# A second feed-forward chunk by seven block products, with the first chunk's up units between them

## The chip, the cores and the metric

The kernel runs on one core of a Trainium2 chip. The metric is device time in microseconds (us) of one execution; lower is better. A profiled execution gives a trace of every engine: TensorE (PE, with its weight loads as PEld), VectorE (DVE), ScalarE (ACT), GpSimd (POOL) and SyncE (SP, which here only issues DMAs).

## The reference

A trunk of two layers over 256 positions of width 1024, float32. Each layer is

```
h = rms_norm(x, ln1_g)
proj = h @ w_in                         # three token mixers and their gates
x = x + merged_mixers(proj) @ w_o
h2 = rms_norm(x, ln2_g)
x = x + (silu(h2 @ w_ff_gate) * (h2 @ w_ff_up)) @ w_ff_down     # 1024 -> 2816 -> 1024
```

The change touches only the last line, the SwiGLU feed-forward part, once in each layer.

## The kernel before

**Precision and products.** Every weight tile and every activation tile is kept as a high and a low part (`wh`, `wl` and `ah`, `al`, both float32r). A 128x128 by 128x512 product is three matmuls: high by high, high by low, low by high (`products`, L308 to L310).

**Weight units.** Weights come in units of 512 KB. SP loads a unit into one of six `st` tiles (L253); ScalarE copies it to `wh` (L272) and VectorE subtracts to get `wl` (L273), each in one of five ring tiles; TensorE then uses it. `loads` is the order of the loads, `cuts` the order of the splits, and both are written out by `plan` before anything else; `take` gives the next unit. A unit of a gate or up projection holds 256 rows by 512 columns and serves 12 matmuls (2 row tiles of 128 positions, 2 row blocks of the weight, 3 matmuls). A unit of the down projection also serves 12.

**The feed-forward part.** Its 2816 hidden columns are five chunks of 512 and one of 256. An ordinary chunk is eight units: four of the gate projection into two PSUM banks, four of the up projection into two more; then silu, the product, four transposes for each row tile and the split into `hsets`. The down units of a chunk follow the gate and up units of the next one (the chunk's hidden part is ready by then). The four down accumulators stand in the four `acc` banks over the whole part; the chunks use the four `tp` banks, except chunk 0, which uses `acc` banks, since the down sums haven't begun.

**Chunks by seven products** (`SEVEN`, chunks 2 and 4 before). Gate and up side by side make a matrix of 2 by 2 blocks (row halves of the weight by gate/up); the activations are 2 by 2 blocks too (two row tiles by two halves of the width). `seven` multiplies these with seven block products instead of eight, in Winograd's form: it needs four combinations of activation blocks (`block_sums`: sums on GpSimd, then splits on ScalarE and VectorE) and four of weight blocks. The weight combinations are made by DMA: base units are loaded (`x` into the two tiles that held `merged`, `y` into those that held `qz`), and GpSimd issues accumulating DMAs that add another block from HBM onto the same tile (L276). The two `x` units are split four times, with one more block added after each of the first three. A block product uses a unit for 6 matmuls. In between, `seven` takes the four down units of the chunk before it at three places: one, two, one.

**What sets the order.** Code is traced in order, with a small list of side tasks (`flow`) that move one step on at each "atom" (6 matmuls); the compiler's scheduler then places each instruction on its engine's queue as early as its operands, its tile and the trace's priorities let it. So a load of the x or y tiles that stands late in the trace can be issued much earlier, once its tile is free. Each engine's queue is then in order.

**Lines that matter here:** L272, L273 the splits; L253 the loads; L276 the accumulating DMAs; L953 and L959 the activation sums, L962 and L963 their splits; L993 the copy of a block sum (`part`), L997, L1014 and L1017 the additions and subtractions of block sums; L977 the hidden product of a seven-product chunk, L929 that of an ordinary one; L336 the transposes; L940 silu.

Of the kernel before, what the change touches and what calls it, by code (L numbers as in the profile page):

```python
# [18 lines left out]
P = 128  # L19
D = 1024  # L20
# [15 lines left out]
NW = 512  # L36
# [4 lines left out]
STAGES = 6  # L41
AHEAD = 5
RING = 5
SEVEN = (2, 4)
LAST = 4

R_CONV, R_CB, R_BA, R_BI, R_LAM, R_SGB, R_QG, R_KG, R_SUB, R_END = (
# [57 lines left out]
def trunk(ctx: ExitStack, tc: tile.TileContext, a: dict, onehot: bass.AP, out: bass.AP):  # L105
# [14 lines left out]
    flow = Flow()  # L120
# [14 lines left out]
    def rows(w, k0, k, c0, c1):  # L135
        return w[k0 * P:(k0 + k) * P, c0:c1].rearrange("(k p) n -> p k n", p=P)
# [14 lines left out]
    def plan(l):  # L151
        def cut(parts):
            cuts.append((unit(parts), []))

        def cols(w, c, n=4):
            for u in range(n):
                cut([(0, NW, rows(w, 2 * u, 2, c * NW, (c + 1) * NW))])

        def down_cut(k):
            cut([(0, D, wd[k * P:(k + 1) * P, :].unsqueeze(1))])  # L160

        def seven(c):

            def half(w, kh):
                return [rows(w, 4 * kh + 2 * u, 2, c * NW, (c + 1) * NW) for u in range(2)]
            b11, b21 = (half(a["w_ff_gate"][l], kh) for kh in range(2))
            b12, b22 = (half(a["w_ff_up"][l], kh) for kh in range(2))
            ks = iter(range(4 * c - 4, 4 * c))
            x = [unit([(0, NW, b11[u])], "merged") for u in range(2)]
            y = [unit([(0, NW, b12[u])], "qz") for u in range(2)]  # L170
            cuts[-1][1].extend((y[u], b22[u]) for u in range(2))
            cuts.extend((x[u], [(x[u], b12[u])]) for u in range(2))
            for u in range(2):
                cut([(0, NW, b21[u])])
            down_cut(next(ks))
            cuts.extend((x[u], [(x[u], b22[u])]) for u in range(2))
            down_cut(next(ks))
            down_cut(next(ks))
            cuts.extend((x[u], [(x[u], b21[u])]) for u in range(2))
            for u in range(2):  # L180
                cut([(0, NW, b22[u])])
            cuts.extend((y[u], []) for u in range(2))
            down_cut(next(ks))
            cuts.extend((x[u], []) for u in range(2))

        w_in, wd = a["w_in"][l], a["w_ff_down"][l]
        for c in (C_XG, C_UV, C_Q, C_K, C_V):
            cols(w_in, c)
        for g in gates_order:
            if isinstance(g, tuple):  # L190
                cols(w_in, C_GATE + 2 * g[0] + g[1])
            else:
                n = int(g[-1])
                cols(a["w_pa"][l], n, 1)
                cols(a["w_pb"][l], n, 1)
                cols(a["w_pc"][l], n, 2)
        for n in range(2):
            cols(a["w_o"][l], n)
        for c in range(nfull + 1):
            if c in SEVEN:  # L200
                seven(c)
                continue
            if c < nfull:
                cols(a["w_ff_gate"][l], c)
                cols(a["w_ff_up"][l], c)
            else:
                lo, hi = c * NW, FFN
                for u in range(4):
                    cut([(0, rest, rows(a["w_ff_gate"][l], 2 * u, 2, lo, hi)),
                         (rest, 2 * rest, rows(a["w_ff_up"][l], 2 * u, 2, lo, hi))])  # L210
            if c:
                for k in range(4 * c - 4, 4 * c):
                    down_cut(k)
        for k in range(4 * nfull, nk_down):
            down_cut(k)
# [93 lines left out]
        nc.tensor.matmul(acc, ah[:, k, :], wl[:, kk, cols], start=False, stop=False, **kw)  # L309
        state["pe"] = nc.tensor.matmul(acc, al[:, k, :], wh[:, kk, cols], start=False, stop=last, **kw).ins  # L310

    def project(sets, nunits, acc):

        for u in range(nunits):
            w = take()
            for r in range(NR):
                for kk in range(2):
                    k = 2 * u + kk
                    products(acc[r], sets[r][k // 4], k % 4, w, kk, slice(0, NW),
                             k == 0, k == 2 * nunits - 1)  # L320
                if r == NR - 1:
                    release()
                atom_done()

    def accs():
        return [acc_bank() for _ in range(NR)]
# [471 lines left out]
    def layer(l, norm1, operands, acc=None):  # L798
# [182 lines left out]
            hsets[c, r] = split(tp, 4)  # L981
            yield 1

        def seven(c):


            (a11, a12), (_, a22) = norm2.sets
            ks = iter(range(4 * c - 4, 4 * c))
            x, w = tp_bank(0), tp_bank(1)

            def copy(bank):
                t = t2k("part")
                nc.scalar.activation(t, bank, AF.Copy)  # L993
                return t

            def gate0(t):
                nc.vector.tensor_tensor(t, t, w, ALU.add)  # L997
                nc.scalar.activation(t, t, AF.Silu, scale=rstd2[0])
                yield 1

            block(x, a11, True)
            g0 = copy(x)
            block(w, a12, True)
            flow.start(gate0(g0))
            down_units([next(ks)])
            z = tp_bank(2)
            block(z, s_ops["s1"], True)
            u1 = copy(z)
            down_units([next(ks)])
            down_units([next(ks)])  # L1010
            block(x, s_ops["s2"], False)
            u0 = copy(x)
            block(z, s_ops["s4"], False)
            nc.vector.tensor_tensor(u0, z, u0, ALU.subtract)  # L1014
            flow.add(half_hidden(c, 0, u0, g0), 1)
            block(x, s_ops["s3"], False)
            nc.vector.tensor_tensor(u1, u1, x, ALU.subtract)  # L1017
            down_units([next(ks)])
            block(x, a22, False)
            g1 = t2k("sg")  # L1020
            nc.scalar.activation(g1, x, AF.Silu, scale=rstd2[1])
            return flow.add(half_hidden(c, 1, u1, g1), 1)
# [24 lines left out]
        def down_units(ks):  # L1047
            if not downs:
                for n in range(2):
                    for r in range(NR):  # L1050
                        downs[r, n] = acc_bank()
            for k in ks:
                w = take()
                for n in range(2):
                    for r in range(NR):
                        down(k, w, r, n)
                    if n == 1:
                        release()
                    atom_done()
# [25 lines left out]
            yield 1  # L1085
            yield from nxt.halves(n)

        flow.add(block_sums(), 18)
        th = None
        for c in range(nfull + 1):  # L1090
            if c in SEVEN:
                th = seven(c)
                continue
            if th is not None and c - 1 in SEVEN:
                before = th
                th = gate_up(c)
                flow.finish(before)
            else:
                th = gate_up(c)
            if 1 <= c < nfull:  # L1100
                down_units(range(4 * c - 4, 4 * c))
                flow.finish(th)
# [171 lines left out]
```

## Time and profile before

| what | value |
|---|---|
| median of 3 runs | 755.29 us (753.62 to 755.35) |
| the profiled execution | 753.26 us, span 751.5 us, granted clock 1.0 |
| TensorE busy | 741.1 us (99%), 3425 matmuls and transposes |
| weight loads busy | 608.3 us (81%) |
| VectorE / ScalarE / GpSimd busy | 530.8 / 438.8 / 148.0 us |
| DMA | 157.70 MB, mean 210 GB/s |

Layer 0's feed-forward part runs from about 199 to 386 us of the span, layer 1's from about 566 us to the end. Busy shares are means over stages with different limits. Matmuls are pipelined, so that their durations overlap; how long a stretch of them takes is read from windows.

### The profile page before, as it was taken

The numbers are of one execution on the slowest core, as the hardware profiler recorded it, in microseconds if no ns is written. First come the engines' busy times: TensorE is split into PE (matmuls) and PEld (weight loads), VectorE is DVE, ScalarE is ACT, GpSimd is POOL, SyncE is SP. The second block draws the span as 40 slices with busy tenths as digits, with TensorE's granted clock in tenths as the row PEclk, the third lists the DMA queues.
The fourth block names the chain that finished last, engine by engine and source line by source line (L and its number), as shares of the span: only waits on it lengthen the run. The fifth ranks groups of instructions, "written<-read, shape, count | busy, mean of one in ns | idle before, by whom it ended". The sixth has DMA issues, their size and how long they took to land.

```text
span 751.5 us, 9745 instructions
## 1 busy us (share of the span) xinstructions
PE 741.1 (99%) x3425; PEld 608.3 (81%) x3425; DVE 530.8 (71%) x749; ACT 438.8 (58%) x647; POOL 148.0 (20%) x163
## 2 busy tenths in 40 slices
PE   8998999999999999999999999999999999999997
PEld 5787888888888887888888788888888888788886
DVE  5788977677785667559577968676866855946772
ACT  5649765454764565457486966554457545745650
POOL 1543010401360211120011420222107211102100
PEclk9999999999999999999999999999999999999999
DMA  6995668677656799888655558776575669997931
GB/s 206 338 313 171 205 191 233 208 218 232 191 167 200 174 239 341 218 213 247 191 175 164 169 166 219 200 225 196 181 240 170 195 171 224 292 314 176 246 116 57
DMA packets 79020, 157.70 MB, mean 210 GB/s; under 512 B 6086, under 2 KB 11836, under 8 KB 78972
## 3 DMA queue, kind: packets, MB, share of 16 engines
q1 hardware_dynamic: 68844, 136.48, 56.3%
q0 software_dynamic: 10128, 20.60, 15.4%
q8 instruction: 27, 0.44, 0.2%
q14 instruction: 21, 0.17, 0.1%
HBM read 156.00 MB, written 1.84 MB: 210 GB/s over the span
## 4 chain that ended last, share of the span: by engine, by line
PE 82%; DVE 6%; DMA 5%; issue 2%; POOL 2%; ACT 2%; SPq 1%; ACTq 0%; DVEq 0%; POOLq 0%
PE acc L310 18%; PE acc L308 18%; PE acc L309 18%; PE tp L308 8%; PE tp L310 8%; PE tp L309 8%; DMA st<-in_w_in_dram 3%; PE tp L336 3%; DVE wl L273 2%; ACT wh L272 2%; PE tp L727 1%; DMA st<-in_w_ff_up_dram 1%; POOL rr L360 1%; DMA st<-in_w_ff_gate_dram 1%; PE tp L762 1%
## 5 line engine op out<-in xcount | busy, mean ns | idle before, releaser
L273 DVE TENSOR_TENSOR wl<-st,wh 128x1024 fp32r<-128x1024 f32 (+1 forms) x277 | 342.3, 1244 | 173.2 <-ACT wh L272 171.8
L272 ACT ACTIVATE wh<-st 128x1024 fp32r<-128x1024 f32 (+1 forms) x277 | 289.5, 1055 | 218.3 <-PE acc L310 119.2
L308 PE MATMUL acc<-wh,ah 128*128 128x512 f32 x704 | 282.4, 401 | 0.0
L310 PE MATMUL acc<-wh,al 128*128 128x512 f32 x704 | 275.3, 391 | 0.0
L309 PE MATMUL acc<-wl,ah 128*128 128x512 f32 x704 | 274.7, 390 | 0.4 <-DVE cqz L468 0.4
L310 PEld LDWEIGHTS acc<-wh,al 128*128 128x128 f32 x704 | 132.1, 188 | 28.2
L309 PEld LDWEIGHTS acc<-wl,ah 128*128 128x128 f32 x704 | 132.5, 188 | 26.3 <-DVE cqz L468 0.9
L308 PEld LDWEIGHTS acc<-wh,ah 128*128 128x128 f32 x704 | 132.3, 188 | 26.0 <-issue 0.6
L308 PE MATMUL tp<-wh,ah 128*128 128x512 f32 x208 | 82.1, 395 | 0.8 <-DVE part L1017 0.8
L310 PE MATMUL tp<-wh,al 128*128 128x512 f32 x208 | 81.1, 390 | 0.0
L309 PE MATMUL tp<-wl,ah 128*128 128x512 f32 x208 | 81.0, 389 | 0.0
L276 POOL DMA_DIRECT2D st<-in_w_ff_up_dram x24 | 28.9, 1222 | 176.5 <-DVE wl L273 163.8
L308 PEld LDWEIGHTS tp<-wh,ah 128*128 128x128 f32 x208 | 39.1, 188 | 8.9 <-issue 1.2
L310 PEld LDWEIGHTS tp<-wh,al 128*128 128x128 f32 x208 | 39.0, 188 | 8.3
L309 PEld LDWEIGHTS tp<-wl,ah 128*128 128x128 f32 x208 | 39.1, 188 | 7.7
L381 POOL TENSOR_TENSOR nss<-nsq 128x1 f32<-128x1 f32 x8 | 3.6, 447 | 123.0 <-ACT junk L377 123.0
L853 POOL TENSOR_TENSOR merged<-merged,tg 128x512 f32<-128x512 f32 x12 | 19.2, 1622 | 39.4 <-DVE tg L850 39.4
L310 PE MATMUL tp<-wh,sl 128*128 128x512 f32 x64 | 25.2, 394 | 0.0
L309 PE MATMUL tp<-wl,sh 128*128 128x512 f32 x64 | 25.2, 394 | 0.0
L308 PE MATMUL tp<-wh,sh 128*128 128x512 f32 x64 | 25.2, 393 | 0.0
L888 POOL DMA_DIRECT2D bg<-in_b_gate_dram x12 | 7.1, 592 | 91.3 <-DVE tg L841 91.3
L342 ACT ACTIVATE ah<-tp 128x512 fp32r<-128x512 f32 (+1 forms) x32 | 17.9, 560 | 9.0 <-PE tp L336 9.0
(203 smaller groups left out, 662.1 us busy)
## 6 DMA issues: line engine op xcount, KB each, us to landing
st<-in_w_in_dram SPq DMA_DIRECT2D x87, 512.0 KB
st<-in_w_ff_down_dram SPq DMA_DIRECT2D x44, 512.0 KB
st<-in_w_ff_up_dram SPq DMA_DIRECT2D x40, 512.0 KB
st<-in_w_ff_gate_dram SPq DMA_DIRECT2D x40, 512.0 KB
st<-in_w_ff_up_dram POOLq DMA_DIRECT2D x24, 512.0 KB, 6.7
st<-in_w_o_dram SPq DMA_DIRECT2D x16, 512.0 KB
st<-in_w_pc_dram SPq DMA_DIRECT2D x8, 512.0 KB
st<-in_w_ff_gate_dram POOLq DMA_DIRECT2D x8, 512.0 KB, 6.2
```

The source lines that it names most:

```text
L272: state["wh"] = nc.scalar.activation(wh[:, k], st[:, k], AF.Copy).ins
L273: state["wl"] = nc.vector.tensor_tensor(wl[:, k], st[:, k], wh[:, k].bitcast(F32), ALU.subtract).ins
L276: nc.gpsimd.dma_start(staged[m], src, accum_op=ALU.add)
L308: nc.tensor.matmul(acc, ah[:, k, :], wh[:, kk, cols], start=first, stop=False, **kw)
L309: nc.tensor.matmul(acc, ah[:, k, :], wl[:, kk, cols], start=False, stop=False, **kw)
L310: state["pe"] = nc.tensor.matmul(acc, al[:, k, :], wh[:, kk, cols], start=False, stop=last, **kw).ins
L336: nc.tensor.transpose(tp[:, (at + j) * P:(at + j + 1) * P], src[:, j * P:(j + 1) * P], ident)
L342: nc.scalar.activation(h_, ps[:, :k * P], AF.Copy)
L360: return nc.gpsimd.tensor_tensor(out_, out_, mhalf[:, :width], ALU.pow).ins
L727: nc.tensor.matmul(tp[:, c, :nk], qz[r][:, c, h, :], kT[:, h, :nk], start=True, stop=True)
L762: nc.tensor.matmul(o_ps[r][:, h * DV:(h + 1) * DV], at[:, j, :], vv[j][:, h * DV:(h + 1) * DV], start=(j == 0), stop=(j == r))
L853: eng.tensor_tensor(m, m, g, ALU.add)
```

## The change

Chunk 1 is made by seven block products too, so that in each layer three chunks of five are. The function takes the weights' quarters and three functions that fill the places between the blocks. For chunk 1 there are no down units of a chunk before it that are ready, so the places are filled with chunk 0's up units: one, three, and then down unit 0; down units 1 to 3 follow after chunk 1, and then chunk 2, by seven products as before. Chunk 0's gate projection now stands alone in front. The activation sums are started at the second atom of the part instead of the eighteenth. The order of loads and splits in `plan` is changed in the same way.

```diff
-SEVEN = (2, 4)
+SEVEN = (1, 2, 4)
...
-        def seven(c):
+        def seven(left, right, fill):
...
             x = [unit([(0, NW, b11[u])], "merged") for u in range(2)]
             y = [unit([(0, NW, b12[u])], "qz") for u in range(2)]
             cuts[-1][1].extend((y[u], b22[u]) for u in range(2))
             cuts.extend((x[u], [(x[u], b12[u])]) for u in range(2))
-            for u in range(2):
-                cut([(0, NW, b21[u])])
-            down_cut(next(ks))
+            for src in b21:
+                cut([(0, NW, src)])
+            for parts in fill[0]:
+                cut(parts)
             cuts.extend((x[u], [(x[u], b22[u])]) for u in range(2))
-            down_cut(next(ks))
-            down_cut(next(ks))
+            for parts in fill[1]:
+                cut(parts)
             cuts.extend((x[u], [(x[u], b21[u])]) for u in range(2))
...
             cuts.extend((y[u], []) for u in range(2))
-            down_cut(next(ks))
+            for parts in fill[2]:
+                cut(parts)
             cuts.extend((x[u], []) for u in range(2))
...
             if c in SEVEN:
-                seven(c)
+                pair = (quarters(a[w][l], c) for w in ("w_ff_gate", "w_ff_up"))
+                if c == 1:
+                    up = [[(0, NW, src)] for src in quarters(a["w_ff_up"][l], 0)]
+                    seven(*pair, (up[:1], up[1:], [down_parts(0)]))
+                    for k in range(1, 4):
+                        down_cut(k)
+                else:
+                    ks = [down_parts(k) for k in range(4 * c - 4, 4 * c)]
+                    seven(*pair, (ks[:1], ks[1:3], ks[3:]))
                 continue
             if c < nfull:
                 cols(a["w_ff_gate"][l], c)
-                cols(a["w_ff_up"][l], c)
+                if c:
+                    cols(a["w_ff_up"][l], c)
...
-        def seven(c):
+        def seven(c, fill):
...
             flow.start(gate0(g0))
-            down_units([next(ks)])
+            fill[0]()
             z = tp_bank(2)
             block(z, s_ops["s1"], True)
             u1 = copy(z)
-            down_units([next(ks)])
-            down_units([next(ks)])
+            fill[1]()
             block(x, s_ops["s2"], False)
...
-            down_units([next(ks)])
+            fill[2]()
             block(x, a22, False)
...
-        flow.add(block_sums(), 18)
-        th = None
-        for c in range(nfull + 1):
+        flow.add(block_sums(), 2)
+        sg0, tasks = [], {}
+        ga = accs()
+        project(norm2.sets, 4, ga)
+        tasks["silu"] = flow.add(silu(ga, NW, sg0))
+        ua = accs()
+
+        def up_units(us):
+            for u in us:
+                project(norm2.sets, 4, ua, only=u)
+
+        def rest_of_up():
+            up_units(range(1, 4))
+            flow.finish(tasks["silu"])
+            tasks["h"] = flow.add(hidden(0, sg0, ua, NW, (3, 1)))
+
+        def first_down():
+            flow.finish(tasks["h"])
+            down_units([0])
+
+        th = seven(1, (lambda: up_units([0]), rest_of_up, first_down))
+        down_units(range(1, 4))
+        for c in range(2, nfull + 1):
             if c in SEVEN:
-                th = seven(c)
+                def down_first(c=c, before=th):
+                    flow.finish(before)
+                    down_units([4 * c - 4])
+                th = seven(c, (down_first, lambda c=c: down_units([4 * c - 3, 4 * c - 2]),
+                               lambda c=c: down_units([4 * c - 1])))
                 continue
```

More of the change, by code (lines that the diff above doesn't have):

```diff
@@ L160, in down_cut @@
             cut([(0, D, wd[k * P:(k + 1) * P, :].unsqueeze(1))])
-        def seven(c):
[L164 to L168, printed above, removed]
+        def seven(left, right, fill):
+            b11, b21 = left[:2], left[2:]
+            b12, b22 = right[:2], right[2:]
             x = [unit([(0, NW, b11[u])], "merged") for u in range(2)]
@@ L172, in seven, with quarters, down_parts @@
             cuts.extend((x[u], [(x[u], b12[u])]) for u in range(2))
-            for u in range(2):
-                cut([(0, NW, b21[u])])
-            down_cut(next(ks))
+            for src in b21:
+                cut([(0, NW, src)])
+            for parts in fill[0]:
+                cut(parts)
             cuts.extend((x[u], [(x[u], b22[u])]) for u in range(2))
-            down_cut(next(ks))
-            down_cut(next(ks))
+            for parts in fill[1]:
+                cut(parts)
             cuts.extend((x[u], [(x[u], b21[u])]) for u in range(2))
-            for u in range(2):
-                cut([(0, NW, b22[u])])
+            for src in b22:
+                cut([(0, NW, src)])
             cuts.extend((y[u], []) for u in range(2))
-            down_cut(next(ks))
+            for parts in fill[2]:
+                cut(parts)
             cuts.extend((x[u], []) for u in range(2))
+        def quarters(w, c):
+            return [rows(w, 2 * u, 2, c * NW, (c + 1) * NW) for u in range(4)]
+        def down_parts(k):
+            return [(0, D, wd[k * P:(k + 1) * P, :].unsqueeze(1))]
         w_in, wd = a["w_in"][l], a["w_ff_down"][l]
@@ L310, in products, with project @@
         state["pe"] = nc.tensor.matmul(acc, al[:, k, :], wh[:, kk, cols], start=False, stop=last, **kw).ins
-    def project(sets, nunits, acc):
-        for u in range(nunits):
+    def project(sets, nunits, acc, only=None):
+        for u in range(nunits) if only is None else (only,):
             w = take()
@@ L982, in half_hidden @@
             yield 1
-        def seven(c):
+        def seven(c, fill):
             (a11, a12), (_, a22) = norm2.sets
-            ks = iter(range(4 * c - 4, 4 * c))
             x, w = tp_bank(0), tp_bank(1)
```

## The prediction

> **What bounds the kernel now.** I read the summary page first (busy shares, the strip of slices, the DMA queues, the chain that ended last, the costliest groups), then the windows of single feed-forward stages, then the chain of waits inside the existing seven-product chunk, then GpSimd's and VectorE's timelines where the change puts new work. The page:
>
> ```profile
> span 751.5 us, 9745 instructions
> PE 741.1 (99%) x3425; PEld 608.3 (81%) x3425; DVE 530.8 (71%) x749; ACT 438.8 (58%) x647; POOL 148.0 (20%) x163
> PEclk9999999999999999999999999999999999999999
> q1 hardware_dynamic: 68844, 136.48, 56.3%
> q0 software_dynamic: 10128, 20.60, 15.4%
> PE 82%; DVE 6%; DMA 5%; issue 2%; POOL 2%; ACT 2%; SPq 1%; ACTq 0%; DVEq 0%; POOLq 0%
> L273 DVE TENSOR_TENSOR wl<-st,wh 128x1024 fp32r<-128x1024 f32 (+1 forms) x277 | 342.3, 1244 | 173.2 <-ACT wh L272 171.8
> L272 ACT ACTIVATE wh<-st 128x1024 fp32r<-128x1024 f32 (+1 forms) x277 | 289.5, 1055 | 218.3 <-PE acc L310 119.2
> L308 PE MATMUL tp<-wh,ah 128*128 128x512 f32 x208 | 82.1, 395 | 0.8 <-DVE part L1017 0.8
> ```
>
> TensorE is busy 99% at full clock and carries 82% of the chain, so time falls only if TensorE gets less to do and is still fed. The last row is the one place where the two seven-product chunks of a layer make it wait: 0.8 us in the whole run. A matmul's 395 ns overlap the next one's, so its price has to be a pitch, which comes from windows (columns: stretch, its length, PE, PEld, DVE, ACT, POOL busy with counts, clock, DMA share, GB/s):
>
> ```profile
> 203.42:221.23 17.81, 17.81 (x81) 14.73 (x80) 14.58 (x18) 12.12 (x18) 14.86 (x9) 1.00 0.54 161
> 255.77:261.21 5.44, 5.44 (x26) 4.51 (x24) 3.40 (x3) 4.61 (x5) 1.18 (x1) 1.00 0.65 206
> 272.17:280.50 8.33, 8.33 (x38) 6.76 (x37) 8.03 (x8) 6.99 (x9) 1.19 (x1) 1.00 0.90 207
> 280.00:288.00 8.00, 7.52 (x35) 6.05 (x34) 7.86 (x9) 5.70 (x8) 2.38 (x2) 1.00 1.05 392
> 316.00:320.00 4.00, 4.00 (x19) 3.32 (x18) 1.45 (x2) 2.06 (x2) 0.09 (x1) 1.00 1.10 190
> 198.60:244.00 45.40, 45.40 (x210) 37.59 (x209) 31.55 (x35) 27.34 (x39) 17.47 (x14) 1.00 0.60 186
> 244.00:304.00 60.00, 59.52 (x270) 48.93 (x269) 40.06 (x39) 34.76 (x39) 9.58 (x8) 1.00 0.94 259
> ```
>
> The second row holds the first 24 matmuls of layer 0's existing seven-product chunk (chunk 2): 5.44/24 = 0.2267 us each. So a weight unit used on all rows (12 matmuls) is 2.72 us of TensorE, a unit of a block product (6 matmuls) 1.36 us. The last two rows show the room: in chunks 0 and 1 of layer 0 the DMA engines are 60% busy, around chunk 2 they are 94% busy, and TensorE still lost only 0.48 us there.
>
> By the Trainium skill, "Perfetto Trace Analysis", section "Identifying the Most-Contended Engine", matmul busy time is no measure of a full TensorE, and weight-load busy is the better one. It is 81% here; if the weight loads set the pace, the 24 matmuls of the second row would be worth their loads alone, 4.51 us in place of 5.44, and the sum below would be 0.9 us smaller. The trace decides for the pitch: no gap stands between those matmuls.
>
> **The change, part by part.** (a) Chunk 1 takes 7 x 12 = 84 matmuls in place of 96, in both layers: -24 x 0.2267 = -5.44 us, all on the path. The eight transposes of its hidden units stay. The third row is the price of block form: 36 block matmuls in 8.33 us, where 36 x 0.2267 is 8.16; so +0.17 a layer, +0.34.
>
> (b) Fourteen units are split into high and low parts instead of eight: 6 x 1.06 us on ScalarE and 6 x 1.24 us on VectorE a layer, and three copies, an add and two subtractions of 0.6 to 0.7 us. Cover: from chunk 0's gate to the end of chunk 2 TensorE will need about 84 us, and VectorE's load rises: from 198.6 to 244 us it is 31.55 of 45.4 us today (69%); 6 splits and 3 further operations of 0.7 make some 9.5 us more in the chunk, most of it in that stretch: some 85 to 90%. Block units are used every 1.36 us and VectorE needs 1.24 of it. There the five units split ahead are the cover, and the three up units in the middle (8.2 us of TensorE, 3.7 of VectorE) refill it. Today's waits in front of chunk 2's last block, in each layer:
>
> ```profile
> 284.30 0.47 PE L308 MATMUL tp<-wh,ah 128*128 128x512 f32 x1 [0.48 <-DVE part L1017]
> 651.86 0.47 PE L308 MATMUL tp<-wh,ah 128*128 128x512 f32 x1 [0.34 <-DVE part L1017]
> ```
>
> Together they are the whole 0.8 us, so chunk 4 has none. VectorE was 98% busy around the first (7.86 of 8.00 us from 280 to 288), so a stretch at 85 to 90% waits about as much: I charge 0.4 us a layer for chunk 1; bounds 0 and 1.2 (one split late in full).
>
> (c) Eight base loads replace eight loads, but eight more come as accumulating DMAs from GpSimd. A plain load is 0.524 MB; at the fourth row's 392 GB/s it takes 1.34 us, at the fifth row's 190 GB/s (accumulating alone) an accumulating one takes 2.76. So a layer's DMA engines get 22 us more work. When today's chunk 2 gets its y base and first y sum, its x bases (two of the six), and how long a transfer takes to land:
>
> ```profile
> 88.33 0.37 SPq L253 DMA_DIRECT2D st<-in_w_ff_up_dram  x1
> 92.83 1.27 POOL L276 DMA_DIRECT2D st<-in_w_ff_up_dram  x1 [1.12 <-PE tp L727]
> 172.65 8.31 SPq L253 DMA_DIRECT2D st<-in_w_ff_gate_dram  x6
> DMA to landing us min/median/max: 5.6/6.3/13.6
> ```
>
> All that is early, as soon as the attention's and the merge's tiles are free, and chunk 1's will be as early. The last line tells of the sums alone (5.6 us at least). What lies on a chain is x: each of its four forms is split, then added to, then split again. Chunk 2's chain of waits (start us, length us, what):
>
> ```profile
> 259.18 1.06 ACT wh L272
> 260.26 1.24 DVE wl L273
> 261.79 8.48 DMA st<-in_w_ff_up_dram
> 270.38 1.07 ACT wh L272
> 271.47 1.24 DVE wl L273
> 272.99 6.33 DMA st<-in_w_ff_gate_dram
> 279.43 1.07 ACT wh L272
> 281.67 0.75 DVE part L977
> 283.47 0.69 DVE part L1017
> 284.30 0.47 PE tp L308
> ```
>
> A step is 2.3 us of splitting and 6.3 to 8.5 us of DMA. In chunk 1 the steps are wider than today's: between the second and third use of x stand three up units, not two down units, so 2.72 + 8.16 = 10.9 us instead of 8.2. With the chunk's gate from 198.6 us (18 matmuls and two groups of transposes before 203.42), and 2.72 us for each block or full unit, chunk 1 runs: x 210.3, b21 213.0, up 0 215.8, x 218.5, ups 221.2, x 229.4, b22 232.1, y 234.9, transposes and down 0 237.6, x 241.4, downs 1 to 3 244.1, chunk 2 from 252.7. A unit is split when the unit five places before it is used up; so x's second form is split from 211.7 and 213.0, the third from 219.9 and 221.2, and with 2.3 us of splitting and 6 to 8 of DMA the sums are there at about 212 (the first form is split at 200 to 204), 223 and 232, and wanted, with the split, at 216, 227 and 239: no wait. Cost 0; without the slack, the late share of one landing, 2 us.
>
> (d) Chunk 2 now follows after only three down units. Its x tiles are free when chunk 1's last form is split, about 236 and 238 to 240 (begun when the b22 units are used up, 233.5 and 234.9); its base lands within some 6 us (a plain load is no slower than a sum's 5.6), is split at 243 to 248, and is wanted at 252.7. Its y base and sums, early today, now fall at 232 to 246, in front of x's first sums. Between 234 and 250 that queues 7 loads and 2 sums (7 x 1.34 + 2 x 2.76 = 15 us of 16), so x's first sums land at about 252 to 257, wanted (with the split) at 258.5 and 259.9: just in time. The second sums then start up to 1 us later against their use than today, where the slack was about 1 us. I charge 0.35 us a layer; bounds 0 and 2.9 (one landing of 8.48 instead of 5.6). If that cover goes, the next late thing is the third sum and then L1017, VectorE's subtraction which today ends the 0.48 us.
>
> (e) The sums of activation halves start at tick 2, not 18. They are wanted sooner: today's first use is in chunk 2, the new one at 218.5 us.
>
> ```profile
> 204.14 6.04 POOL L953 TENSOR_TENSOR sum<-ah,al 128x512 f32<-128x512 f32 x4
> 210.26 8.34 POOL L959 TENSOR_TENSOR sum<-sum 128x512 f32<-128x512 f32 x4
> 246.76 1.26 POOL L276 DMA_DIRECT2D st<-in_w_ff_up_dram  x1 [28.17 <-DVE wl L273]
> 208.93 2.33 DVE L273 TENSOR_TENSOR wl<-st,wh 128x1024 fp32r<-128x1024 f32 x1 [1.15 <-ACT wh L272]
> 212.20 1.29 DVE L273 TENSOR_TENSOR wl<-st,wh 128x1024 fp32r<-128x1024 f32 x1 [0.94 <-ACT wh L272]
> 214.37 1.37 DVE L273 TENSOR_TENSOR wl<-st,wh 128x1024 fp32r<-128x1024 f32 x1 [0.87 <-ACT wh L272]
> 215.66 3.48 DVE L963 TENSOR_TENSOR sl<-sum,sh 128x512 fp32r<-128x512 f32 x2
> ```
>
> GpSimd starts them as early as it can already, at 204.14; the first operand, s1, is complete after the first half of the last row, 217.4, though its difference was done at about 212.4. So it makes 218.5 even in today's order. Two accumulating issues (1.2 us each) now stand in GpSimd's queue in front of or among the sums, and behind them wait the other differences (wanted from 229 on). They cost nothing while the 1.9 us hold in which s1 lay finished before it was split. Charge 0, bounds 0 and 1.3.
>
> (f) The ring's SP issues: b21 and up units swap places, the second set of x loads waits on SP for the split of the first, with down and gate loads behind it. These are five to six units ahead of use; nothing.
>
> Sum: -5.44 + 0.34 + 2 x 0.4 + 2 x 0.35 = -3.6 us. The profiled execution took 753.26 us (span 751.5 and 1.8 around it): 749.7. It lies 2.0 below the median of the three runs, 755.29 (they reach from 753.62 to 755.35); against that median, 751.7.
>
> **Rivals.** (1) The x chain of chunk 2 loses what chunk 1 gains: if both of its middle sums land 2 us late in each layer, the stalls are some 2 x 2 us instead of 0.7, and the time is 755. For it speaks that chunk 2 is the only place with a wait today and that its DMA engines are 94% busy; against it that chunk 4, with the same chain at 316 to 350 us, has no wait at all.
>
> (2) Slower: the DMA engines become the bound from chunk 0's gate to chunk 2's end. That stage needs 28 plain loads and 14 accumulating ones, 28 x 1.34 + 14 x 2.76 = 76 us of the 84 us that TensorE takes. But the accumulating ones rarely run at their best: a lone one takes 5.6 us to land from its issue, and if each effectively takes 4 us the stage is 94 us long. The eight or nine units loaded ahead repay about 5 of these 10 us, the other 5 stall TensorE in each layer: 755.3 - 3.6 + 10 = 762. It decides from an effective price of about 3.3 us (84 us) upward. For it: 0.94 of share in the last windows row was reached with 18 loads and 8 sums, 46 us of work by the best prices in 60. Against it: TensorE still ran through there.
> The Trainium skill, "DMA: Bandwidth & Descriptors", section "Issuing engines are not separate DMA queues", says that transfers issued from different engines run on the same 16 engines and interleave, which speaks for this rival; the trace agrees, with 1.05 and 1.10 of share in the windows where loads and sums pile up.
>
> (3) s1 is late: VectorE and GpSimd slow each other while the sums run (2.33 us instead of 1.24 for the split at 208.93), and two accumulating issues come first. If all of it goes through, TensorE waits 1.3 us a layer more: 754.3.
> The Trainium skill, "SBUF — State Buffer", section "Who interferes with whom", has it that a VectorE operation with two SBUF inputs contends with a GpSimd operation that reads SBUF, the later one blocking. The trace agrees at 208.93, but the next two splits took 1.29 and 1.37 us beside the differences.
>
> **How the numbers follow.** The forecast has 0.63, rival 1 has 0.19, rival 2 has 0.11, rival 3 has 0.07. What this kernel's measurement can tell from no change is about 0.3%, 2.3 us. The forecast's own range is 748.5 to 753 (the full 5.4 us and today's waits gone, with some scatter, at the low end; twice the charges of (b) and (d) at the high end), and is faster. Rivals 1 and 3 lie within 0.3% but for 0.03 on the faster side and 0.01 on the slower; rival 2 is slower. So faster 0.66, same 0.22, slower 0.12. The range 748.2 to 756.2 takes in the forecast and most of rivals 1 and 3; it leaves out rival 2.
>
> **What would show it.** TensorE has 24 instructions fewer (3401) and about 5 us less busy time. (b), (e): no idle time before s1's first block and before chunk 1's last block. (c): chunk 1's x sums land before 212, 223 and 232 or so, and no wait for them by ScalarE leads on to TensorE. (d): waits on L1017 stay under 1 us a layer, and the DMA share over 198 to 283 us lies between 0.8 and 1. The prediction is wrong if TensorE's idle time in the two layers' feed-forward parts grows by over 2 us, or if chunk 2's own stretch is longer than today's 31 us by more than a microsecond.

## The result, and the profile after

The changed kernel is slower: 772.0 us (median of 4 runs, 771.43 to 774.98) against 755.14 us (4 runs, 753.62 to 755.35). The ratio is 1.024, 95% interval 1.0226 to 1.0254. The profiled execution took 771.43 us, span 769.6. In the changed kernel the lines of before stand 15 further down (13 in the last lines of `seven`): L287 and L288 are the splits, L291 the accumulating DMA, L323 to L325 the three matmuls, L351 the transposes, L968 and L974 GpSimd's activation sums, L977 and L978 their splits, L992 and L944 the hidden products, L1030 the last subtraction.

The page of the changed kernel:

```profile
span 769.6 us, 9801 instructions
PE 743.4 (97%) x3401; PEld 605.2 (79%) x3401; DVE 551.4 (72%) x767; ACT 450.8 (59%) x665; POOL 162.1 (21%) x179
q0 software_dynamic: 14480, 28.99, 21.4%
PE 68%; DMA 11%; DVE 9%; POOL 4%; issue 4%; ACT 3%; SPq 1%; ACTq 0%; DVEq 0%; POOLq 0%
```

The matmuls did go (3401 instructions, 24 fewer), and TensorE's share of the chain fell from 82% to 68%: DMA, GpSimd and ScalarE now stand on it. What TensorE waits for (total us, times, longest):

```profile
PE tp L324 <- DVE wl L288: 5.7, 6, 1.4
PE tp L323 <- ACT wh L287: 4.0, 4, 2.0
PE tp L351 <- DVE sg L944: 3.0, 2, 1.5
PE tp L323 <- DVE part L1030: 2.4, 3, 1.0
PE acc L324 <- DVE wl L288: 2.3, 2, 1.2
```

These five are 17.4 us; before, the feed-forward parts had 0.8. In the stages of layer 0, and in the last row one of layer 1 (columns as in the prediction):

```profile
198.60:283.00 84.40, 75.69 (x334) 60.11 (x333) 58.63 (x60) 49.45 (x67) 30.44 (x27) 1.00 0.87 218
213.50:220.80 7.30, 4.79 (x20) 3.27 (x20) 7.30 (x6) 7.29 (x10) 4.11 (x4) 1.00 0.44 143
220.80:246.00 25.20, 23.69 (x109) 18.93 (x107) 20.08 (x23) 16.03 (x20) 5.00 (x5) 1.00 0.97 258
246.00:258.00 12.00, 11.33 (x53) 9.35 (x53) 9.52 (x11) 6.45 (x8) 3.24 (x3) 1.00 1.09 295
258.00:292.00 34.00, 29.98 (x121) 23.42 (x120) 19.74 (x20) 18.00 (x20) 4.91 (x5) 0.95 0.92 233
282.25:285.60 3.35, 3.35 (x9) 2.63 (x8) 3.35 (x4) 3.35 (x6) 0.40 (x1) 0.50 0.70 103
657.75:661.16 3.41, 3.41 (x10) 2.63 (x9) 3.41 (x4) 3.41 (x5) 0.87 (x1) 0.50 0.60 74
```

TensorE is idle 8.7 us in 84.4, in three places. I call them A (213.5 to 220.8: 2.8 us in each layer, counted as the time by which the starts of matmuls lie further apart than their pitch), B (220.8 to 250: 2.5 us in each layer) and C (258 to 292: 4.9 us in layer 0, 3.9 in layer 1). The last two rows are a cost of C that is no waiting: after it, in each layer, TensorE runs at a clock of 0.50 for some 3.4 us; nine matmuls fill 3.35 us in which 14.8 would fit at 0.2267. Sum over both layers, with 1.2 us in chunk 4: 20.7 us of waits, less 1.2 counted so in the kernel before, plus 3.0 us of half clock more than before, less 5.4 for the matmuls: +17.1. Measured: +18.1 in the spans, +16.9 in the medians.

**A.** The timeline of the changed kernel from 204 to 214 us (start us, length us, in brackets the idle time before it and what ended it), ScalarE, then VectorE, then GpSimd:

```profile
204.22 1.06 ACT L287 ACTIVATE wh<-st 128x1024 fp32r<-128x1024 f32 x1 [0.25 <-PE acc L325]
211.12 0.63 ACT L977 ACTIVATE sh<-sum 128x512 fp32r<-128x512 f32 x1 [5.84 <-POOL sum L974]
205.31 4.63 DVE L288 TENSOR_TENSOR wl<-st,wh 128x1024 fp32r<-128x1024 f32 x1 [0.18 <-ACT wh L287]
212.94 2.31 DVE L288 TENSOR_TENSOR wl<-st,wh 128x1024 fp32r<-128x1024 f32 x1
204.65 4.19 POOL L968 TENSOR_TENSOR sum<-ah,al 128x512 f32<-128x512 f32 x3
208.93 7.47 POOL L974 TENSOR_TENSOR sum<-sum 128x512 f32<-128x512 f32 x4
```

GpSimd adds without a gap from 204.65 to 216.4. VectorE's subtraction for a low part, which has a median of 1.23 us, takes 4.63 beside it, and another 2.31. ScalarE does nothing for 5.84 us: the split of the first activation sum is next in its queue and waits for GpSimd, and the splits of ready weight units stand behind it. So two units are late, and TensorE waits for their low parts.
The Trainium skill, "SBUF — State Buffer", section "Who interferes with whom", calls the port pair that VectorE and GpSimd share an exclusive lock, taken by whoever issues first. The trace agrees: the subtraction begins inside the first of the three sums of the fifth row and ends at 209.94, 1.1 us after the last of them. It was held up by the whole run of sums and not by one of them.

**B and C.** The chain of waits of the changed kernel:

```profile
219.54 1.15 POOL st L291
220.69 10.08 DMA st<-in_w_ff_up_dram
230.85 1.07 ACT wh L287
235.44 1.32 DVE sg L944 x2
252.94 14.25 DMA st<-in_w_ff_up_dram
267.26 1.07 ACT wh L287
268.36 1.24 DVE wl L288
269.88 8.85 DMA st<-in_w_ff_up_dram
278.84 1.07 ACT wh L287
279.93 1.24 DVE wl L288
282.42 0.43 PE tp L325
```

B: chunk 1's second x sum is issued at 219.5, after GpSimd's sums, and takes 10.08 us to land. ScalarE waits 3.9 us for it with the b22 splits behind, VectorE's hidden product of chunk 0 (L944) waits in turn, and TensorE then waits for that product before its transposes. C: chunk 2's first x sum lands after 14.25 us and the second after 8.85. In front of them stand chunk 2's own y sums. GpSimd's accumulating DMAs:

```profile
244.32 1.18 POOL L291 DMA_DIRECT2D st<-in_w_ff_up_dram  x1 [9.67 <-DVE wl L288]
245.67 1.19 POOL L291 DMA_DIRECT2D st<-in_w_ff_up_dram  x1 [0.17 <-issue]
250.98 1.19 POOL L291 DMA_DIRECT2D st<-in_w_ff_up_dram  x1 [4.13 <-DVE wl L288]
252.94 1.19 POOL L291 DMA_DIRECT2D st<-in_w_ff_up_dram  x1 [0.77 <-DVE wl L288]
```

The first two are y, issued at 244.3 and 245.7 and landed at 254.3 and 258.7; the other two are x, landed at 262.7 and 267.2. From 246 to 258 us the share of the DMA engines is 1.09.

### The profile page after: what moved, and what is told of

It is laid out like the page before. It is cut to its first block, busy times and chain, and to the rows that moved or that the text cites. A ratio compares the mean times of both kernels' runs of the same rounds, so it can differ in the third digit from the quotient of the medians.

```text
span 769.6 us, 9801 instructions
## 1 busy us (share of the span) xinstructions
PE 743.4 (97%) x3401; PEld 605.2 (79%) x3401; DVE 551.4 (72%) x767; ACT 450.8 (59%) x665; POOL 162.1 (21%) x179
## 3 DMA queue, kind: packets, MB, share of 16 engines
q0 software_dynamic: 14480, 28.99, 21.4%
## 4 chain that ended last, share of the span: by engine, by line
PE 68%; DMA 11%; DVE 9%; POOL 4%; issue 4%; ACT 3%; SPq 1%; ACTq 0%; DVEq 0%; POOLq 0%
PE acc L324 15%; PE acc L325 15%; PE acc L323 15%; DMA st<-in_w_ff_up_dram 7%; PE tp L324 6%; PE tp L323 6%; PE tp L325 5%; DVE wl L288 5%; PE tp L351 3%; ACT wh L287 2%; DMA st<-in_w_in_dram 2%; PE tp L742 1%; POOL sum L974 1%; POOL sum L968 1%; POOL rr L375 1%
## 5 line engine op out<-in xcount | busy, mean ns | idle before, releaser
L288 DVE TENSOR_TENSOR wl<-st,wh 128x1024 fp32r<-128x1024 f32 (+1 forms) x289 | 361.9, 1264 | 167.1 <-ACT wh L287 162.0
L287 ACT ACTIVATE wh<-st 128x1024 fp32r<-128x1024 f32 (+1 forms) x289 | 300.3, 1054 | 218.3 <-PE acc L325 111.4
L323 PE MATMUL acc<-wh,ah 128*128 128x512 f32 x704 | 282.2, 401 | 0.0
L325 PE MATMUL acc<-wh,al 128*128 128x512 f32 x704 | 275.3, 391 | 0.0
L325 PEld LDWEIGHTS acc<-wh,al 128*128 128x128 f32 x704 | 132.1, 188 | 28.2
L323 PEld LDWEIGHTS acc<-wh,ah 128*128 128x128 f32 x704 | 132.3, 188 | 26.2 <-issue 0.6
L291 POOL DMA_DIRECT2D st<-in_w_ff_up_dram x36 | 43.3, 1203 | 163.5 <-DVE wl L288 129.6
L323 PE MATMUL tp<-wh,ah 128*128 128x512 f32 x168 | 66.4, 395 | 2.4 <-DVE part L1030 2.4
L324 PE MATMUL tp<-wl,ah 128*128 128x512 f32 x168 | 65.6, 391 | 2.7 <-DVE wl L288 2.7
L325 PE MATMUL tp<-wh,al 128*128 128x512 f32 x168 | 65.6, 390 | 0.0
L323 PE MATMUL tp<-wh,sh 128*128 128x512 f32 x96 | 40.0, 416 | 4.0 <-ACT wh L287 4.0
L324 PE MATMUL tp<-wl,sh 128*128 128x512 f32 x96 | 39.5, 411 | 3.0 <-DVE wl L288 3.0
L325 PE MATMUL tp<-wh,sl 128*128 128x512 f32 x96 | 39.0, 406 | 0.0
L323 PEld LDWEIGHTS tp<-wh,ah 128*128 128x128 f32 x168 | 31.6, 188 | 9.4 <-DVE part L1030 1.8
L325 PEld LDWEIGHTS tp<-wh,al 128*128 128x128 f32 x168 | 31.5, 188 | 6.7
L323 PEld LDWEIGHTS tp<-wh,sh 128*128 128x128 f32 x96 | 18.7, 195 | 9.8 <-ACT wh L287 5.7
L291 POOL DMA_DIRECT2D st<-in_w_ff_gate_dram x12 | 14.3, 1189 | 54.7 <-DVE wl L288 51.2
```

The costliest lines, as they stand in the source:

```text
L287: state["wh"] = nc.scalar.activation(wh[:, k], st[:, k], AF.Copy).ins
L288: state["wl"] = nc.vector.tensor_tensor(wl[:, k], st[:, k], wh[:, k].bitcast(F32), ALU.subtract).ins
L291: nc.gpsimd.dma_start(staged[m], src, accum_op=ALU.add)
L323: nc.tensor.matmul(acc, ah[:, k, :], wh[:, kk, cols], start=first, stop=False, **kw)
```

## The experiments

Each is the changed kernel with the edit shown, in one run beside a run of the kernel before on the same chip, unless more is said; such pairs are read to about 2 us. Much of that lies ahead of layer 0's feed-forward part, which begins at 199.6 us in one run of the last kernel below and at 201.9 in another. Where less is at stake I give the length of the two feed-forward parts together: each from the start of the last residual addition ahead of it (L911 before, L926 in the changed kernel) to that of its own last one (L1084, L1097), in layer 1 to the end of the span. It is 370.9 us in the kernel before and 389.9 in the changed one, and is read to about 1 us. Line numbers move by up to three between them. Waits of TensorE without a row are counted from the starts of its matmuls, as above.

**The start of the activation sums (A).**

```diff
-        flow.add(block_sums(), 2)
+        flow.add(block_sums(), 8)
```

> The activation sums are started at tick 8 instead of 2; nothing else changes. Theory A (ScalarE's queue stands behind the split of s1, which waits for GpSimd, and VectorE's split is held up by GpSimd's sums): the waits at 213 and 216 us and their like in layer 1 (5.7 us in both layers) go, and with them most of the late second sums of chunk 1 and the 3.3 us before the transposes of chunk 0; chunk 2's waits (8.8 us and 3 us of half clock) stay: some 763 us. Rival D (the accumulating transfers are too many for the DMA engines, wherever the sums stand): only the 5.7 us at most go, 766 us or more. Rival A-only (all waits follow from the first ones, which put everything late): all go, some 752 us.

765.52 us (before: 753.99). A's two waits and B's are gone, and there is a new one instead:

```profile
PE tp L325 <- DVE sl L978: 6.4, 2, 3.2
```

The sums are now themselves late, 3.4 us a layer by the starts of the matmuls, with 3.41 us at half clock behind it; of C's waits 1.0 us is left in layer 0 and 2.2 in layer 1. The run tells something else of A. Three of GpSimd's sums and two differences still run back to back, from 206.45 to 215.14 us, and VectorE's splits from 200 to 222 us are still stretched (shortest, median, longest in ns):

```profile
L288 DVE TENSOR_TENSOR wl<-st,wh x9: 1211/1227/4637, 200.7 to 220.2; 128x1024 fp32r<-128x1024 f32 x9
```

TensorE does not wait for any of them. What is gone is ScalarE's wait for the first activation sum: its split now stands at 217.88, behind the weight units' splits. So the stretched split alone does not make A; A needs the wait at the head of ScalarE's queue. With tick 5:

> As changed, but the sums start at tick 5, between the changed kernel's 2 and the 8 that was tried. With tick 2 ScalarE's splits wait behind s1's split (2.8 us a layer), with tick 8 s1 is split too late (3.4 us a layer). Theory A with the port held by GpSimd's sums as the root: no tick helps, between 2 and 3.4 us a layer stay at one place or the other, 764 to 770 us. Rival (only the order in ScalarE's queue matters): a middle place has neither wait, 760 us.

773.64 us (before: 756.19), more than expected, with A as in the changed kernel. The scheduler put GpSimd's sums where they were (205.16 to 216.89 us, the run being 0.5 us later throughout), so no place in between was tried. Of the two places seen on GpSimd neither is free: early the sums stand in the way, late they are missing. What tells whether GpSimd is the cause is to take them off it:

```diff
-                    nc.gpsimd.tensor_tensor(t[r, n], ah.bitcast(F32), al.bitcast(F32), ALU.add)
+                    nc.vector.tensor_tensor(t[r, n], ah.bitcast(F32), al.bitcast(F32), ALU.add)
...
-                nc.gpsimd.tensor_tensor(t[o], t[p], t[q], op)
+                nc.vector.tensor_tensor(t[o], t[p], t[q], op)
```

> As changed, but the eight activation sums and differences run on VectorE instead of GpSimd (5.5 us of VectorE a layer). Theory A (GpSimd's sums hold up VectorE's splits, and ScalarE's queue stands behind the split of a late s1): the two waits before and in the first up unit (5.7 us in both layers) go, no wait takes their place at s1's block, the splits there take 1.24 us again, and the late hidden product of chunk 0 (3.3 us) goes with them: 762 to 764 us, with chunk 2's waits left. Rival V (VectorE is simply too full there): 5.5 us more work make it worse, 771 us or more.

764.12 us (before: 756.19). A is gone, though VectorE has eight operations more to do. The splits from 200 to 222 us, in the changed kernel and then in this one:

```profile
L288 DVE TENSOR_TENSOR wl<-st,wh x8: 1210/1226/4627, 198.9 to 220.9; 128x1024 fp32r<-128x1024 f32 x8
```

```profile
L288 DVE TENSOR_TENSOR wl<-st,wh x10: 1219/1221/1227, 199.9 to 221.5; 128x1024 fp32r<-128x1024 f32 x10
```

None is stretched any more, ten instead of eight begin in those 22 us, and ScalarE waits for no sum. B (2.0 us a layer) and C stay (8.3 us of waits in both layers, and the half clock).

**Chunk 2's y sums (C).** First the neighbour taken away: chunk 2 made in the ordinary way, `SEVEN = (1, 4)`, with as many products as before the change.

> Chunks 1 and 4 by seven products, chunk 2 by eight; as many matmuls as in the kernel before the change. Theory A with C (chunk 2's waits come from its sums queueing behind other transfers right after chunk 1): chunk 1's waits stay (5.7 + 3.3 + 1.7 us), those of chunk 2 and the half clock are gone, and the kernel before's own 0.8 us too: 755 + 10 = 765 us. Rival D: without chunk 2's eight sums the DMA engines have room, so that chunk 1's late sums and the 5 us behind them go too: about 760 us.

765.74 us (before: 753.99). A and B as in the changed kernel, no wait in chunk 2, no half clock. Then chunk 2 by seven products without its y sums:

```diff
-            cuts[-1][1].extend((y[u], b22[u]) for u in range(2))
+            if add_y:
+                cuts[-1][1].extend((y[u], b22[u]) for u in range(2))
...
-                    seven(*pair, (ks[:1], ks[1:3], ks[3:]))
+                    seven(*pair, (ks[:1], ks[1:3], ks[3:]), c != 2)
```

> As changed, but chunk 2's y tiles don't get their accumulating transfers (one of the four weight combinations of chunk 2 is left out, two transfers a layer). Theory C (x's first sums wait behind the two y sums): x's first sums land 5 to 6 us earlier, and most of chunk 2's 8.8 us of waits and the 3 us of half clock go: 760 to 763 us. Rival D: two sums of 16 a layer less give 2 x 2.8 us of transfer a layer, and the waits shrink by at most that in proportion, 1 to 2 us: 769 us or more. Rival A-only: no change, 771 us.

764.0 us (before: 753.99). The stretch of C, which had 29.98 us of TensorE in 34:

```profile
258.00:292.00 34.00, 33.81 (x152) 27.62 (x151) 24.43 (x24) 21.22 (x24) 7.17 (x7) 1.00 0.98 256
```

C and the half clock are gone; A and B are there. Its x sums landed in 6.3 and 7.7 us instead of 11.7 and 14.3. Next, all transfers kept but y in tiles of its own, so that base and sums can come long before. Tried first for chunk 2 alone:

```diff
-            y = [unit([(0, NW, b12[u])], "qz") for u in range(2)]
+            y = [unit([(0, NW, b12[u])], ys_) for u in range(2)]
...
-                    seven(*pair, (ks[:1], ks[1:3], ks[3:]))
+                    seven(*pair, (ks[:1], ks[1:3], ks[3:]), *(('merged', 'y2') if c == 2 else ()))
```

> As changed, but chunk 2's y tiles are two tiles of their own, so that their base loads and sums can go much earlier, when other transfers leave room; the number of transfers is that of the changed kernel. Theory C: as without the y sums, 760 to 763 us. Rival D in its strict form (sum of transfers in the feed-forward part): the same gain, since they leave that part; then it differs from C only in the kernel without the y sums and in the spaced chunks. Rival A-only: 771 us.

778.0 us (before: 753.99), a miss: the scheduler moved chunk 4's y units, whose tiles were now free at 236 us, into the very place of chunk 2's, and x's first sums again took 11.5 and 14.1 us. So it said nothing on C but that any y transfer at that place will do. With own tiles for chunks 2 and 4:

> As changed, sums on GpSimd at tick 2, but chunks 2 and 4 share two y tiles of their own. In the earlier try, with own tiles for chunk 2 alone, chunk 4's y loads and sums took the freed tiles of chunk 1 and stood at the same place. Theory C: now nothing but x's sums stands there, as in the kernel without chunk 2's y sums: 763 to 765 us, with chunk 1's waits left. Rival D: 769 us or more.

770.95 us (before: 756.19). By the time alone that is rival D's, yet C's waits are gone in both layers. With the sums on VectorE as well:

> Both: sums on VectorE, and chunks 2 and 4 share two y tiles of their own, so that chunk 2's y base and sums can be moved as early as chunk 1's. If A and C are the two causes and independent: chunk 1's waits and most of chunk 2's go, the 5.4 us of removed matmuls come to light, and the time is 750 to 753 us, below the kernel before. Rival D (the x sums alone are too many between chunk 0 and chunk 3): chunk 2 keeps 2 us or more of waits a layer, 755 us or more.

763.75 us (before: 756.19), again on rival D's side by the time alone. The same stretch of the latter:

```profile
258.00:292.00 34.00, 34.00 (x152) 27.96 (x151) 26.10 (x25) 23.00 (x26) 7.15 (x6) 1.00 1.00 276
```

C is gone with every transfer still made: it is a matter of order, not of traffic. Layer 0's feed-forward part takes 184.8 us, 6.4 less than with the sums on VectorE alone. But both kernels gave the gain back in layer 1's chunk 4: a last accumulating DMA of 11.0 us instead of 6.7 to 7.0 kept TensorE 5.3 us (in the waits: `PE tp L349 <- DVE part L990`, 3.8, and L1028 behind it), and 6.83 us at half clock followed.

**B, and what a seven-product chunk is worth.** Chunks 1 and 4, with the sums on VectorE:

> Chunks 1 and 4 by seven products (as many products as the kernel before), activation sums on VectorE. Theory (three separate stalls: A from the GpSimd sums, B from the late second x sum of chunk 1, C from chunk 2's y sums in front of its x sums): A and C cannot occur, only B is left, some 2.1 us a layer, so 755 - 1.0 (the waits of today's chunk 2) + 4.2 = 757 to 760. Rival (a seven-product chunk in place 1 is slow as such, whatever engine makes the sums): as with the sums on GpSimd, 765.

757.86 us (before: 756.75): only B is left, 1.8 us a layer. And the kernel before with one seven-product chunk less:

```diff
-SEVEN = (2, 4)
+SEVEN = (4,)
```

> The kernel before with chunk 4 alone by seven products: what one such chunk really saves. By the pitch of 0.2267 us, 12 matmuls in each layer come back, +5.4 us, and the two waits of 0.5 go: 754 + 4.4 = 758 to 759. If the price of a matmul in the prediction was too high (weight loads of 0.19 us set the pace), +4.5 - 1 = 757.5; if a seven-product chunk saves nothing because of its own extra work, 754.

758.9 us (before: 756.75). Its feed-forward parts take 374.8 us, 3.9 more than in the kernel before: that is what one chunk saves in both layers, where the terms are 5.4 for the matmuls less 0.3 for the block form and 1.2 for the waits that go. Then B itself: with all four up units between s1's block and s2's, the second x sum gets 2.7 us more.

```diff
-                    seven(*pair, (up[:1], up[1:], [down_parts(0)]))
+                    seven(*pair, ([], up, [down_parts(0)]))
...
-            up_units(range(1, 4))
+            up_units(range(4))
...
-        th = seven(1, (lambda: up_units([0]), rest_of_up, first_down))
+        th = seven(1, (lambda: None, rest_of_up, first_down))
```

> The changed kernel with the activation sums on VectorE and all four of chunk 0's up units in one place, behind the s1 block (before: one in front of it, three behind). The second form of x is then used 2.7 us sooner and its third form 10.9 us later instead of 8.2. Theory: the second x sum has 2.7 us more time, so B (1.2 + 0.8 us of waits in layer 0) goes; C stays: 764 - 4 = 760. It could turn over if the first x sum or s1 is then late (they have some 2 us to spare): then 764 to 766. Rival (B comes from VectorE being full and not from the sum's landing): B stays, 764.

757.42 us (before: 756.75), 2.6 us better than expected. B is gone in both layers. C alone is left, and it is smaller than it was, which the expectation did not have: 4.0 us of waits in both layers, where the sums on VectorE alone left 8.3, and no half clock.

```profile
PE tp L323 <- ACT wh L287: 1.9, 3, 0.8
PE tp L324 <- DVE wl L288: 1.8, 3, 0.8
```

**All three taken away.** The last kernel, and chunk 2's and 4's y units in memory that two tiles of the mixers (`kT`, `u`) leave free:

```diff
-            y = [unit([(0, NW, b12[u])], "qz") for u in range(2)]
+            y = [unit([(0, NW, b12[u])], ys[u]) for u in range(2)]
...
-                    seven(*pair, (ks[:1], ks[1:3], ks[3:]))
+                    seven(*pair, (ks[:1], ks[1:3], ks[3:]), ("kT", "u"))
...
-        u_n = work.tile([P, NR, SGW], F32, tag="u", name="u")
+        u_n = work.tile([P, 2 * NR, SGW], F32, tag="u", name="u")[:, :NR]
```

> As the one with all four up units in one place, and the y units of chunks 2 and 4 in tiles of their own, which share memory with two tiles of the mixers, so that chunk 2's y base and sums land before chunk 1 begins. Theory: A, B and C are all taken away, so the gain of 5.4 us shows: 754 - 1 - 5.4 + 1 for what is left = 748 to 751. Rival (VectorE is too full for three seven-product chunks, or another wait comes in the place of each): 756 to 762. A late last accumulating DMA in layer 1's chunk 4, as seen with own y tiles, would add some 5 us.

753.51 us (before: 756.75), above the expected range. Timed in five rounds:

> The version with all three stalls taken away, timed against the kernel before. Theory (nothing else stands against the 24 matmuls that go): 5.4 us less, of which 1.28 and 0.97 us of waits in front of a chunk's last block were seen to stay against today's 1.0, and the rest of the single run's 3 us lay in the start, where the kernels do the same: a ratio of 0.992 to 0.996. If the 2.8 us of TensorE waiting at 50 to 60 us in that run belong to the kernel, 0.996 to 0.998; rival (the sum of small new waits eats the gain): 0.998 to 1.002.

751.02 us (749.38 to 753.36) against 754.76 (752.66 to 756.86): ratio 0.9947, interval 0.9928 to 0.9966. It beats both kernels, the one before by 0.5%. Its page, two rows of its waits, and the stretch that had 75.69 us of TensorE in 84.4:

```profile
span 749.3 us, 9794 instructions
PE 737.1 (98%) x3401; PEld 604.1 (81%) x3401; DVE 548.7 (73%) x783; ACT 452.0 (60%) x665; POOL 138.3 (18%) x163
q0 software_dynamic: 14480, 28.99, 22.0%
```

```profile
PE tp L322 <- ACT ah L356: 1.1, 1, 1.1
PE tp L322 <- DVE part L1029: 1.1, 2, 0.6
```

```profile
198.00:283.00 85.00, 84.47 (x383) 69.02 (x381) 67.91 (x78) 58.21 (x76) 17.36 (x19) 1.00 0.90 229
```

The same 3401 instructions and the same 28.99 MB of accumulating transfers as in the changed kernel take 21 us less. VectorE is busy 80% there, the DMA engines 90%, and TensorE loses 0.5 us, and 0.6 more just behind, as the wait in front of chunk 2's last block goes on to 283.66. By the two rows 2.2 us of waits are left in front of the last blocks, 1.4 more than before the change; -5.4 + 0.3 (block form) + 1.4 gives -3.7. Measured: -3.7 in the medians, -3.0 in the feed-forward parts.

**Put back one at a time.** The last kernel with the sums on GpSimd:

> The version with all three stalls taken away, but the activation sums back on GpSimd: stall A alone. Theory (A is worth its waits in the changed kernel, 2.83 us a layer, and needs nothing else): 753.5 + 5.7 = 758 to 760, with the two waits on VectorE's split of the low part at 213 to 217 us back and none at chunk 2's x units. Rival (A only hurt because B and C followed, or the four up units hide it): 753 to 755. As s1 is now used 2.7 us sooner it could also cost more, up to 763.

764.34 us, above all that was expected.

```profile
PE tp L323 <- DVE wl L287: 2.7, 3, 1.4
PE tp L350 <- DVE sg L943: 1.5, 1, 1.5
PE tp L322 <- DVE part L1029: 1.2, 2, 0.7
```

These are the waits from 198 to 300 us: A, and in the second and third row B, back at full size although the four up units still stand together. The second x sum is issued at 222.3 instead of 217.4 and takes 11.60 us. So A makes B: GpSimd's sums hold up the split of x's second form, and with it the next sum. The feed-forward parts are 12.0 us longer than in the kernel without A; the rest of the 13.3 us lies ahead of them. And with one and three up units again, the sums on VectorE:

> The version with all three stalls taken away, but chunk 0's up units one and three again: stall B alone. Theory: some 2.1 us a layer at the transposes of chunk 0 and the block behind, as with the sums on VectorE: 753.5 + 4 = 757 to 758.5. Rival (B comes and goes with chunk 2's transfers): 753 to 755.

754.52 us, in the rival's range by the time alone. But B's waits are there, 1.8 us in each layer (0.99 at the transposes, 0.84 at the block behind, in layer 0). The feed-forward parts are 1.9 us longer, as most of the waits in front of chunk 2's and 4's last blocks fall away in exchange; the rest of the 3.5 us over 751.02 lies ahead of them, in the start of that run.

The feed-forward parts of both layers together:

| kernel | us |
|---|---|
| before the change | 370.9 |
| changed | 389.9 |
| all three taken away (two runs) | 367.9 and 368.1 |
| A put back | 380.0 |
| B put back | 369.8 |
| C left (757.42) | 372.7 |

So A, with the B that it makes, costs 12.0 us, B by the order of the up units alone 1.9, and C alone 4.7: 18.6 of the 21.9 us by which the changed kernel is longer. The rest is not split up any further. C alone has 4.0 us of waits and no half clock; in the changed kernel it has 8.8, and 3.0 of half clock behind it.

## Why the prediction was wrong

It said 751.7 us, range 748.2 to 756.2; 772.0 was measured. The steps that failed are (c), (d) and (e).

(a) The saving held: 3401 instructions, and once nothing else stood in the way the kernel ran at 751.0.

(b) held in size. The wait that it names, in front of chunk 1's last block, came at 0.71 us in each layer (it is counted in B): charged 0.4, bound 1.2. It went by load (85 to 90% busy), and load was not the limit: with eight operations more on VectorE, A disappeared. What it left out is that a split can last 4.63 us. The 2.33 us of the split at 208.93 stood in the prediction's own rows, and was taken for the worst case. By itself this cost nothing: with the sums from tick 8 a split of 4.64 us stands at the same place and TensorE does not wait.

(c) failed: "no wait". The sums of x were to land at about 212, 223 and 232; the second landed at 230.8. Issue and landing were both wrong: it was issued at 220.7 for the supposed 216 or so, because the split in front of it was held up by A, and took 10.08 us instead of 6 to 8, behind the first sum and beside the ring's loads. That is B, 2.5 us a layer. The landing is the larger part: with A gone the sum was issued at 217.8, took 10.28 us, and 2.0 us a layer were left.

(d) failed in size. The mechanism is the one described (y sums and loads in front of x's first sums); the landing was put at 252 to 257 us and came at 262.7 and 267.2. The sum of 15 us of transfers was set into a window from 234 to 250, but the y sums could not be issued before their base had landed, at 243.8 and 245.1. Charged 0.35 a layer, bound 2.9; measured 4.9 and 3.9, and 3.0 us of half clock in both layers together, which no term had.

(e) failed in what it looked at. It asked whether s1 would be in time for its own use, and it was. It kept the order of ScalarE's queue, where s1's split stood behind the weight units' splits, after s1 was done. Asked for at tick 2, that split moved ahead of them, and they stood behind it while ScalarE waited 5.84 us for GpSimd; two of them came too late for TensorE. That is A, 2.8 us a layer against bounds of 0 and 1.3.

(f) "nothing" cannot be told apart: SP's loads are among what the second x sum shared the DMA engines with, and no run moved them alone.

**The rivals.** Rival 1 named C's mechanism at less than half its size (4 us of waits in both layers for 8.8). Rival 2 named the slower side but not the cause: the DMA engines are no bound, as the version at 751.0 moves the same bytes at a share of 0.90. Rival 3 named A's place, at 1.3 us for 2.8, but as a lateness of s1 itself, which was in time. What failed above all is that they were taken as alternatives with a chance each: A delays the sums of B, and all came together. The prediction's own signs were clear: idle time in the feed-forward parts grew by some 19 us where 2 were allowed. The share of the DMA engines, 0.87, lay in the range given and told nothing.

## What to carry to other kernels

When a side computation on GpSimd is moved earlier, price not only whether its result is in time but what stands behind the instruction that waits for it on ScalarE's in-order queue, and count VectorE's two-input operations beside back-to-back GpSimd work at several times their length (4.63 us for 1.22 here). When two chunks with the same chain of transfers come next to each other, list the issue times of both chains, with the earliest time that each operand allows; a transfer that used to be early because its tile was idle will land in front of the one that is urgent. Tiles for the early transfer, taken from memory that an earlier stage has left, undid that at no cost in traffic.

## What the runs showed of the hardware

- A VectorE subtraction of 128x1024 took 4.63 us beside three GpSimd additions in a row, and 1.22 us without them.
- A lone accumulating DMA of 512 KB landed in 5.6 to 6.0 us; one issued within some 2 us behind another, among more or fewer plain loads, in 7.2 to 14.3 us. The Trainium skill, "DMA: Bandwidth & Descriptors", section "Issuing engines are not separate DMA queues", has transfers of all engines interleave on the same 16 engines; the 10.08 us of the second x sum, with nothing but plain loads beside it and one sum ahead, agree.
- After C TensorE ran at half clock for 3.41 us in each layer. The two waits just before it were 2.2 and 1.0 us in layer 0, and 1.05 and 1.03 us in layer 1, with a single matmul between. With the four up units together a pair of 0.97 and 1.03 us at the same place in layer 1 left the clock as it was, so the lengths alone do not decide. The Trainium skill, "TensorE: Matmul & The Clock Gate", section "What's actually happening", puts the drop after an idle window of about 3.4 us; here it came behind a pair of waits of little over 1 us each.
- With y tiles of their own, the last accumulating DMA of layer 1 took 11.0 us, twice, where GpSimd and SP issued within 0.01 us of each other (715.77 and 715.76 us in one, 708.62 both in the other), 9.9 us in a third such case (725.22 and 725.21), and 6.7 to 7.0 us where SP came 0.3 us behind. Whether that coincidence is the cause was not tried.
